# Half of the contraction of x @ w_ffn_in as 2x2 Strassen products in a float32 transformer trunk

## The chip, the cores and the metric

The kernel runs on one core of one Trainium2 chip. The metric is the device time of one execution in microseconds (us); lower is better. Engines: PE is TensorE's matmul stream, PEld its weight loads, DVE is VectorE, ACT is ScalarE, POOL is GpSimd, SP is SyncE, which here only issues transfers.

## The reference

Two layers of a streaming-encoder trunk on 256 tokens of width 2048, in float32. Each layer mixes tokens by three attention branches, merges them by gates, projects, normalizes, and then runs the feed-forward part:

```python
f_gate, f_up = jnp.split(x @ w_ffn_in[l], 2, axis=-1)      # w_ffn_in[l]: 2048 x 11264
x = layer_norm(DEEPNORM_ALPHA * x + (jax.nn.silu(f_gate) * f_up) @ w_ffn_out[l], ln2_g[l], ln2_b[l])
```

The hidden width is 5632, so `f_gate` and `f_up` are 11 chunks of 512 columns each.

## The kernel before

Every float32 product is made of three passes in float32r, TensorE's reduced float32 format: an operand w is split into h (w rounded) and l (w - h, rounded), and xh*wh + xh*wl + xl*wh accumulate in PSUM. One matmul takes 128 rows of the contraction (a k-tile), 128 tokens as the stationary operand and 512 weight columns as the moving one. The 256 tokens are two token tiles.

`gemm` computes 512 output columns for both token tiles in two PSUM banks. It goes over the contraction in units of two k-tiles. For each unit `load_unit` issues one transfer of 512 KB from DRAM on SP's queue into a `raw` buffer (5 of them), ACT rounds it into `wh` (L64) and DVE subtracts to get `wl` (L65); 6 buffers each of `wh` and `wl`. Then TensorE runs 12 matmuls of the unit (2 k-tiles x 2 token tiles x 3 passes, L90 to L92). A `gemm` over all 2048 rows is 8 units and 96 matmuls.

The feed-forward part goes over the 11 hidden chunks f in groups of 4, 4 and 3. For each f there is one `gemm` for the gate columns (L510), then sigmoid on ACT (L514) and a product on DVE (L515); one `gemm` for the up columns (L517), a product on DVE (L520), and 4 + 4 transposes on TensorE (L124, `hidTp`), split again into `rh` and `rl` (L52, L53). After a group, four `gemm`s multiply the hidden chunks by w_ffn_out. The text calls the gate `gemm` and the up `gemm` of one f, with what follows them, a **pair**: 192 matmuls and 8 transposes. There are 11 pairs in a layer and 22 in the kernel.

Each engine runs its instructions in the order in which they are put down; a scheduler sets that order when the program is built, and waits are semaphores. So an instruction that waits holds up everything behind it on its engine.

Of the kernel before, what the change touches and what calls it, by code (L numbers as in the profile page):

```python
# [29 lines left out]
UK = 2  # L30
# [3 lines left out]
def trunk_kernel(ctx: ExitStack, tc: tile.TileContext, x, w_in, sinks, lq1, lk1, lq2, lk2, diff_g,  # L34
                 rel_bias, w_br_a, w_br_b, w_br_c, w_gate, b_gate, w_out, ln1_g, ln1_b,
                 w_ffn_in, w_ffn_out, ln2_g, ln2_b, cos_a, sin_a, cos_b, sin_b, out):
    """Float32 products run as three float32r passes: w = h + l exactly, with h and l the
    float32r roundings of w and of w - h; xh*wh + xh*wl + xl*wh accumulate in PSUM."""
# [20 lines left out]
    def load_unit(src, k0, c0):  # L59
# [7 lines left out]

    side = []

    def pump():  # L70
        """one more stage of the work that runs beside the products"""
# [47 lines left out]
    def transpose4(src, name):  # L119
        """[128 tok, 4*128] -> PSUM [128, 4, 128 tok]"""  # L120
# [6 lines left out]
    # ---------------------------------------------------------------- constants  # L127
# [22 lines left out]
    # additive masks, [128 q, (keys of query tile 0: 128 | keys of query tile 1: 256)]  # L150
# [12 lines left out]
    for layer in range(DEPTH):  # L163
        lam_init = 0.8 - 0.6 * math.exp(-0.3 * layer)

        # ------------------------------------------------------------ q / k / v
        def head_slots(reg, i0, n):
            """n slots of [128, 256], two in each of the tiles reg{i0}, reg{i0+1}, .."""
# [3 lines left out]
        def rope(src, cos, sin, nh, hd):  # L172
            """src PSUM [128 tok, nh*hd] -> SBUF, rotated"""
# [45 lines left out]
        # ------------------------------------------------------------ attention of a pair of maps  # L219
        def exps(qs, ks, scale, bias, sk=None):  # L220
            """qs, ks: two [d, 256] operands, bias: additive, [128, 384] each; sk: sink columns.
            Returns exp(s - max) [128 q, 2, (k0 of q0 | k0 k1 of q1)] and the reciprocal sums [128, t, m]."""
            e = scr.tile([P, 2, 3 * P], F32, tag="e", name="e", bufs=2)
# [24 lines left out]
            return seg, rs  # L248
# [5 lines left out]
        def transposed(seg, n):  # L254
            """probabilities of n maps, key-major: [128 keys, n, 3, 128]: (q0,k0), (q1,k0), (q1,k1)"""
            pT = scr.tile([P, 2, 3, P], F32, tag="pT", name="pT", bufs=2)
# [6 lines left out]
            return pT  # L263

        def pv_heads(seg, rs, vs, yh, yl, i0):
# [3 lines left out]
            pT = transposed(seg, 2)  # L269
# [11 lines left out]
        def attn_a(h0, aq, ak, av, yh, yl):  # L281
            kv = h0 // 4
            seg, rs = exps([aq[h0], aq[h0 + 1]], [ak[kv]] * 2, P ** -0.5, [mask_a] * 2, slice(h0, h0 + 2))
            yield from pv_heads(seg, rs, [av[kv]] * 2, yh, yl, h0 % 4)

        def attn_c(h0, cq, ck, cv, yh, yl):
            seg, rs = exps([cq[h0], cq[h0 + 1]], [ck[h0], ck[h0 + 1]], P ** -0.5,
                           [relb[:, h0 + i, :] for i in range(2)])
            yield from pv_heads(seg, rs, [cv[h0], cv[h0 + 1]], yh, yl, h0)

        def attn_b(h, bq, bk, bv, yh, yl):
            seg, rs = exps([bq[h][0:64], bq[h][64:128]], [bk[h][0:64], bk[h][64:128]], 64 ** -0.5, [mask_b] * 2)
# [6 lines left out]
            pT = transposed(seg, 1)  # L299
# [27 lines left out]
        # ------------------------------------------------------------ branch A  # L327
# [11 lines left out]
        # ------------------------------------------------------------ small per-layer values  # L339
# [22 lines left out]
        # relb[p, h, :]: rel_bias[h, 256 + t - u] with the chunk mask, laid out as the masks.  # L362
        # raw[p, c] = rel_bias[h, 129 + p + c], so raw[p, 255 - c] = rel_bias[h, 384 + p - c].
# [21 lines left out]
        # ------------------------------------------------------------ branch B  # L385
# [9 lines left out]
        # ------------------------------------------------------------ branch C  # L395
# [10 lines left out]
        # ------------------------------------------------------------ gates, branch projections, merge  # L406
# [33 lines left out]
        # ------------------------------------------------------------ layer norm  # L440
# [27 lines left out]
        # ------------------------------------------------------------ output projection, residual, norm  # L468
# [25 lines left out]
        # ------------------------------------------------------------ feed-forward  # L494
# [10 lines left out]
        groups = [range(0, 4), range(4, 8), range(8, NFC)]  # L505
        stats = new_stats()
# [76 lines left out]
```

## Time and profile before

| | |
|---|---|
| Time, median of 3 runs | 2859.63 us (2859.13 to 2859.66) |
| Profiled execution, first to last instruction | 2858.1 us |
| Busy: PE, PEld | 2828.1 us, 2332.2 us |
| Busy: DVE, ACT, POOL | 1624.8 us, 1243.3 us, 60.5 us |
| Moved by DMA | 549.17 MB |
| Granted TensorE clock, mean | 0.999 |

The span of the profiled execution is 1.5 us short of the median of the runs; what lies around the span is start and end. PE's busy time is not a measure of its peak, since matmuls are pipelined and their ends are modelled: one matmul of 512 columns is recorded as some 390 ns, and the next starts long before it ends. How many matmuls start in a stretch says more.

### The profile page before, as it was taken

To read this page: it belongs to the slowest core of one execution; us is meant where nothing else is said; L and a number is where in the kernel's file an instruction comes from. 1 tells how busy PE (TensorE), PEld (TensorE's weight loads), DVE (VectorE), ACT (ScalarE), POOL (GpSimd) and SP (SyncE) were. 2 spreads that over 40 slices of the span, in tenths; PEclk is the share of its full clock that TensorE was granted. 3 is DMA by queue.
4 is the path that set the end of the run, shared out by engine and by line. 5 is a ranking of instruction groups with operands and counts; after the bars stand their busy time and mean duration, and the time that the engine had idled before them with its cause. 6 is when DMAs were issued, how large, how long until landed. Compare 5 with 4: busy or idle time off the path is not lost. (4 is left out here: it accounts for less than half of the span.)

```text
span 2858.1 us, 33530 instructions
## 1 busy us (share of the span) xinstructions
PE 2828.1 (99%) x12840; PEld 2332.2 (82%) x12840; DVE 1624.8 (57%) x1816; ACT 1243.3 (44%) x1590; POOL 60.5 (2%) x110
## 2 busy tenths in 40 slices
PE   8999999999999999999999999999999999999998
PEld 6888888887888888888878888888878888888886
DVE  5656556566555455555576565556575555554555
ACT  4455444443444444344345454444444434443442
POOL 0000000000000000000000000000000000000000
PEclk9999999999999999999999999999999999999999
DMA  7555666665655555566564556666656556555653
GB/s 252 170 162 174 206 201 202 198 226 175 219 190 192 192 190 190 191 190 198 183 214 152 179 180 199 203 201 206 212 198 191 190 191 195 186 190 192 192 191 125
DMA packets 282656, 549.17 MB, mean 192 GB/s; under 512 B 19840, under 2 KB 21376, under 8 KB 282496
## 3 DMA queue, kind: packets, MB, share of 16 engines
q1 hardware_dynamic: 276096, 526.07, 56.7%
q0 software_dynamic: 6400, 20.98, 2.5%
q8 instruction: 100, 1.64, 0.2%
q14 instruction: 60, 0.49, 0.0%
HBM read 542.78 MB, written 4.19 MB: 191 GB/s over the span
## 5 line engine op out<-in xcount | busy, mean ns | idle before, releaser
L65 DVE TENSOR_TENSOR wl<-raw,wh 128x1024 fp32r<-128x1024 f32 x992 | 1212.1, 1224 | 1129.3 <-ACT wh L64 1128.7
L64 ACT CAST wh<-raw 128x1024 fp32r<-128x1024 f32 x992 | 1044.7, 1054 | 1478.7 <-PE acc L92 1369.0
L90 PE MATMUL acc<-wh,xh 128*128 128x512 f32 x2752 | 1082.2, 393 | 8.4 <-ACT xh L52 8.3
L92 PE MATMUL acc<-wh,xl 128*128 128x512 f32 x2752 | 1076.1, 391 | 0.2 <-DVE xl L53 0.2
L91 PE MATMUL acc<-wl,xh 128*128 128x512 f32 x2752 | 1073.9, 390 | 2.1 <-DVE wl L65 1.9
L90 PEld LDWEIGHTS acc<-wh,xh 128*128 128x128 f32 x2752 | 517.5, 188 | 117.3 <-ACT xh L52 10.6
L91 PEld LDWEIGHTS acc<-wl,xh 128*128 128x128 f32 x2752 | 517.8, 188 | 109.5 <-DVE wl L65 4.7
L92 PEld LDWEIGHTS acc<-wh,xl 128*128 128x128 f32 x2752 | 517.4, 188 | 109.1 <-DVE xl L53 2.2
L92 PE MATMUL acc<-wh,rl 128*128 128x512 f32 x1216 | 474.4, 390 | 0.0
L90 PE MATMUL acc<-wh,rh 128*128 128x512 f32 x1216 | 474.2, 390 | 0.0
L91 PE MATMUL acc<-wl,rh 128*128 128x512 f32 x1216 | 473.5, 389 | 0.0
L92 PEld LDWEIGHTS acc<-wh,rl 128*128 128x128 f32 x1216 | 228.3, 188 | 47.3
L91 PEld LDWEIGHTS acc<-wl,rh 128*128 128x128 f32 x1216 | 228.3, 188 | 46.9
L90 PEld LDWEIGHTS acc<-wh,rh 128*128 128x128 f32 x1216 | 228.3, 188 | 46.9
L239 ACT ACTIVATE e<-e,nm 128x128 f32<-128x128 f32 (+1 forms) x80 | 35.4, 444 | 23.9 <-DVE nm L233 23.9
L459 POOL TENSOR_TENSOR rstd<-rstd,mhalf 128x1 f32<-128x1 f32 x8 | 7.7, 966 | 1585.6 <-DVE rstd L458 1585.6
L514 ACT ACTIVATE sig<-acc 128x512 f32<-128x512 f32 x44 | 26.3, 598 | 23.4 <-PE acc L92 21.6
L515 DVE TENSOR_TENSOR sig<-sig,acc 128x512 f32<-128x512 f32 x44 | 30.1, 688 | 7.8 <-ACT sig L514 7.8
L420 DVE TENSOR_TENSOR gate<-acc,bg 128x512 f32<-128x512 f32 x48 | 31.0, 683 | 1.2 <-PE oT L319 1.1
L52 ACT CAST xh<-xTp 128x512 fp32r<-128x512 f32 x32 | 17.7, 588 | 31.4 <-PE xTp L124 31.0
L53 DVE TENSOR_TENSOR rl<-hidTp,rh 128x512 fp32r<-128x512 f32 x44 | 28.2, 682 | 0.0
L520 DVE TENSOR_TENSOR sig<-sig,acc 128x512 f32<-128x512 f32 x44 | 28.1, 680 | 0.0
(123 smaller groups left out, 822.9 us busy)
## 6 DMA issues: line engine op xcount, KB each, us to landing
raw<-in_w_ffn_in_dram SPq DMA_DIRECT2D x352, 512.0 KB, 3.4
raw<-in_w_gate_dram SPq DMA_DIRECT2D x192, 512.0 KB, 4.3
raw<-in_w_ffn_out_dram SPq DMA_DIRECT2D x176, 512.0 KB, 3.5
raw<-in_w_in_dram SPq DMA_DIRECT2D x144, 512.0 KB, 3.6
raw<-in_w_out_dram SPq DMA_DIRECT2D x64, 512.0 KB, 4.0
raw<-in_w_br_a_dram SPq DMA_DIRECT2D x32, 512.0 KB, 4.1
raw<-in_w_br_b_dram SPq DMA_DIRECT2D x16, 512.0 KB, 4.7
raw<-in_w_br_c_dram SPq DMA_DIRECT2D x16, 512.0 KB, 4.8
```

Source lines behind the costliest of these rows:

```text
L52: nc.scalar.copy(h, src)
L53: nc.vector.tensor_sub(l, src, h.bitcast(F32))
L64: nc.scalar.copy(h, raw)
L65: nc.vector.tensor_sub(l, raw, h.bitcast(F32))
L90: nc.tensor.matmul(acc[t], ah, wh[:, j, :], start=kt == 0, stop=False)
L91: nc.tensor.matmul(acc[t], ah, wl[:, j, :], start=False, stop=False)
L92: nc.tensor.matmul(acc[t], al, wh[:, j, :], start=False, stop=kt == nk - 1)
L239: nc.scalar.activation(seg[t][:, m, :], seg[t][:, m, :], AF.Exp, bias=nm[:, t, m:m + 1], accum_out=sm[:, t, m:m + 1])
L420: nc.vector.tensor_add(g, acc[t], bg)
L514: nc.scalar.activation(s, accg[t], AF.Sigmoid)
L515: nc.vector.tensor_mul(s, s, accg[t])
L520: nc.vector.tensor_mul(sg[t], sg[t], accu[t])
```

## The change

For the pairs f = 1 to 10 of each layer (20 in all; f = 0 stays as it was) the two `gemm`s become one `pair_gemm`. It takes the gate columns N1 and the up columns N2 of the weights together, as the two column blocks of a 2x2 block product; the two token tiles are the two row blocks.

The contraction's 16 k-tiles are four chunks of 4. Chunks 0 and 2 (`cs`) go by the Winograd form of Strassen's product: 7 block products of 128 tokens x 2 k-tiles x 512 columns in place of 8. Chunks 1 and 3 (`cp`) go plainly (`four`), into the same PSUM banks, and where a bank holds a combination they use the sum that it calls for (one difference of token tiles per chunk). One chunk of each kind makes a **block** of the text; a pair is two blocks. TensorE works through the units of a block in this order, each with 6 matmuls, those written with "plain" 12:

u (u0, product p7), f1 (plain), p1, H1 (hub, q5), f2 (plain), p3 (b22), H2 (hub, p6), f3 (plain), p2, f4 (plain), H3 (hub, q4).

That is 11 units and 90 matmuls. The weight sums: `T` ("hub") is loaded on SP's queue, DVE adds it to b22 (`u0`, L599), and then three DMAs on POOL's queue with an add (`grow`, L603, 512 KB each) turn it into the next sums in place. A `grow` waits until DVE has read T for the product before; the split of T for the next product waits until the `grow` has landed. Two T buffers alternate between blocks.

The sums of x are made once per layer (`x_sums`), beside the plain pair f = 0. At the end of a pair seven DVE additions and one ACT copy turn seven PSUM banks into the four results; all eight banks are in use (four tags `acc`, four `aux`). The groups of hidden chunks are 3, 3, 3 and 2, in place of 4, 4 and 3. To make room, the buffers of the attention probabilities share one tag (`att`), which `u0` uses too, and the last `gemm`'s `tail` is 8 in both layers.

```diff
+    def block(src, k0, c0):
+        return src[k0 * P:(k0 + UK) * P, c0:c0 + CW].rearrange("(k p) n -> p k n", p=P)
+    def load_raw(src, k0, c0):
         raw = wpool.tile([P, UK, CW], F32, tag="raw", name="raw", bufs=5)
+        nc.sync.dma_start(raw, block(src, k0, c0))
+        return raw
+    def split_unit(raw):
         h = wpool.tile([P, UK, CW], F32R, tag="wh", name="wh", bufs=6)
         l = wpool.tile([P, UK, CW], F32R, tag="wl", name="wl", bufs=6)
-        nc.sync.dma_start(raw, src[k0 * P:(k0 + UK) * P, c0:c0 + CW].rearrange("(k p) n -> p k n", p=P))
         nc.scalar.copy(h, raw)
         nc.vector.tensor_sub(l, raw, h.bitcast(F32))
         return h, l
...
+        def pair_gemm(src, n1, n2):
+            bank = {}
+            for k in ("p3", "p7", "q5", "q4"):
+                bank[k] = psA.tile([P, CW], F32, tag="acc", name=k)
+            for k in ("p1", "p6", "p2"):
+                bank[k] = psX.tile([P, CW], F32, tag="aux", name=k)
...
+            def prod(k, lhs, w):
+                for j in range(UK):
+                    (ah, al), (wh, wl) = lhs(j), w
+                    nc.tensor.matmul(bank[k], ah, wh[:, j, :], start=k not in begun, stop=False)
+                    begun.add(k)
+                    nc.tensor.matmul(bank[k], ah, wl[:, j, :], start=False, stop=False)
+                    todo[k] -= 1
+                    nc.tensor.matmul(bank[k], al, wh[:, j, :], start=False, stop=todo[k] == 0)
...
+            for i in range(2):
+                cs, cp = 2 * i, 2 * i + 1
+                k1, k2, kp = 4 * cs, 4 * cs + 2, 4 * cp
...
+                T = act.tile([P, UK, CW], F32, tag=("rh3", "rl3")[i], name="hub")
+                nc.sync.dma_start(T, block(src, k1, n2))
+                b22 = load_raw(src, k2, n2)
+                u0 = scr.tile([P, UK, CW], F32, tag="att", name="u0", bufs=2)
+                nc.vector.tensor_add(u0, T, b22)
+                prod("p7", s3, split_unit(u0))
+                def grow(kr, c0):
+                    nc.gpsimd.dma_start(T, block(src, kr, c0), accum_op=ALU.add)
+                def four(j0, c0, ks):
+                    w = load_unit(src, kp + j0, c0)
+                    for k, (h, l) in ks:
+                        prod(k, part(h, l, j0), w)
...
+                N2 = (("q5", X[1]), ("p3", sums[cp][0]))
+                N1 = (("p2", X[0]), ("q4", X[1]))
+                grow(k1, n1)
+                four(0, n2, N2)
+                prod("p1", A[0][0], load_unit(src, k1, n1))
+                prod("q5", s1, split_unit(T))
+                grow(k2, n2)
+                four(2, n2, N2)
+                prod("p3", s4, split_unit(b22))
+                prod("p6", s2, split_unit(T))
+                grow(k2, n1)
+                four(0, n1, N1)
+                prod("p2", A[0][1], load_unit(src, k2, n1))
+                four(2, n1, N1)
+                prod("q4", A[1][1], split_unit(T))
+            p1, v, y, c22 = tmp("p1"), tmp("v"), tmp("y"), tmp("c22")
+            nc.scalar.copy(p1, bank["p1"])
+            nc.vector.tensor_sub(v, bank["p6"], p1)
+            nc.vector.tensor_sub(y, bank["p7"], v)
+            nc.vector.tensor_add(v, bank["q5"], v)
+            nc.vector.tensor_sub(c22, v, bank["p7"])
+            nc.vector.tensor_add(v, bank["p3"], v)
+            nc.vector.tensor_add(p1, bank["p2"], p1)
+            nc.vector.tensor_add(y, bank["q4"], y)
+            return [p1, y], [v, c22]
...
-        groups = [range(0, 4), range(4, 8), range(8, NFC)]
+        groups = [range(0, 3), range(3, 6), range(6, 9), range(9, NFC)]
...
+        side.append(x_sums())
...
-                accg = gemm(w_ffn_in[layer], 0, 16, f * CW, x_lhs)
                 sg = []
+                if f == 0:
+                    accg = gemm(w_ffn_in[layer], 0, 16, f * CW, x_lhs)
+                else:
+                    drain()
+                    accg, accu = pair_gemm(w_ffn_in[layer], f * CW, FFN + f * CW)
```

The order on the engines, at three places. First DVE at the seam between the pairs f = 1 and f = 2 of layer 0. Before, the splits (L65) of two `gemm`s follow on one another, with the two products L520 and the splits `rl1` of the hidden chunk between them:

```order
L65 TENSOR_TENSOR wl_6219<-raw_6217,wh_6218 128x1024
L65 TENSOR_TENSOR wl_6237<-raw_6235,wh_6236 128x1024
L520 TENSOR_TENSOR sig_5991<-sig_5991,acc_5997 128x512
L520 TENSOR_TENSOR sig_5994<-sig_5994,acc_5998 128x512
L65 TENSOR_TENSOR wl_6255<-raw_6253,wh_6254 128x1024
L53 TENSOR_TENSOR rl1_6144<-hidTp_6146,rh1_6143 128x4x128
L53 TENSOR_TENSOR rl1_6144<-hidTp_6154,rh1_6143 128x4x128
L65 TENSOR_TENSOR wl_6273<-raw_6271,wh_6272 128x1024
```

Now, from the last split of the first pair (H3, on `hub_6050`) to the one that waits for its last matmul (L635, on bank q4), the seven additions stand between the splits of the next pair's units u, f1, p1 and H1 (on `u0_6252`, `raw_6265`, `raw_6283`, `hub_6248`):

```order
L73 TENSOR_TENSOR wl_6196<-hub_6050,wh_6195 128x1024
L73 TENSOR_TENSOR wl_6255<-u0_6252,wh_6254 128x1024
L629 TENSOR_TENSOR v_6206<-p6_5893,p1_6205 128x512
L73 TENSOR_TENSOR wl_6268<-raw_6265,wh_6267 128x1024
L630 TENSOR_TENSOR y_6207<-p7_5889,v_6206 128x512
L631 TENSOR_TENSOR v_6206<-q5_5890,v_6206 128x512
L73 TENSOR_TENSOR wl_6286<-raw_6283,wh_6285 128x1024
L632 TENSOR_TENSOR c22_6208<-v_6206,p7_5889 128x512
L634 TENSOR_TENSOR p1_6205<-p2_5894,p1_6205 128x512
L633 TENSOR_TENSOR v_6206<-p3_5888,v_6206 128x512
L73 TENSOR_TENSOR wl_6296<-hub_6248,wh_6295 128x1024
L635 TENSOR_TENSOR y_6207<-q4_5891,y_6207 128x512
```

What moved: six of the seven additions and four splits of the next pair now stand ahead of the first instruction that needs the end of this pair.

Second, DVE inside a pair, after the seam. Before, only splits of freshly loaded `raw` tiles:

```order
L65 TENSOR_TENSOR wl_6273<-raw_6271,wh_6272 128x1024
L65 TENSOR_TENSOR wl_6291<-raw_6289,wh_6290 128x1024
L65 TENSOR_TENSOR wl_6317<-raw_6315,wh_6316 128x1024
L65 TENSOR_TENSOR wl_6335<-raw_6333,wh_6334 128x1024
L65 TENSOR_TENSOR wl_6353<-raw_6351,wh_6352 128x1024
```

Now, from the pair's first block after H2 (units f3, p2, f4) through its second block's H2 (on `hub_6403` the second time); L599 is the next block's `u0`:

```order
L73 TENSOR_TENSOR wl_6348<-raw_6345,wh_6347 128x1024
L73 TENSOR_TENSOR wl_6366<-raw_6363,wh_6365 128x1024
L73 TENSOR_TENSOR wl_6378<-raw_6375,wh_6377 128x1024
L599 TENSOR_TENSOR u0_6407<-hub_6403,raw_6405 128x1024
L73 TENSOR_TENSOR wl_6394<-hub_6248,wh_6393 128x1024
L73 TENSOR_TENSOR wl_6410<-u0_6407,wh_6409 128x1024
L73 TENSOR_TENSOR wl_6423<-raw_6420,wh_6422 128x1024
L73 TENSOR_TENSOR wl_6441<-raw_6438,wh_6440 128x1024
L73 TENSOR_TENSOR wl_6451<-hub_6403,wh_6450 128x1024
L73 TENSOR_TENSOR wl_6464<-raw_6461,wh_6463 128x1024
L73 TENSOR_TENSOR wl_6480<-raw_6405,wh_6479 128x1024
L73 TENSOR_TENSOR wl_6490<-hub_6403,wh_6489 128x1024
```

What moved: between the splits on one hub (`hub_6403`, H1 and then H2) there are two splits on `raw` tiles, and L599 stands ahead of the H3 of the block before it.

Third, SP's queue at the same pair. Before, one load for each unit, in the units' order:

```order
L63 DMA raw_6125<-in_w_ffn_in_dram 128x2x512
L63 DMA raw_6163<-in_w_ffn_in_dram 128x2x512
L63 DMA raw_6181<-in_w_ffn_in_dram 128x2x512
L63 DMA raw_6199<-in_w_ffn_in_dram 128x2x512
L63 DMA raw_6217<-in_w_ffn_in_dram 128x2x512
```

Now, from the second block's b22 (`raw_6052`) to the next pair's b22 (`raw_6250`); `hub_6248` is the next pair's first T:

```order
L66 DMA raw_6052<-in_w_ffn_in_dram 128x2x512
L66 DMA raw_6067<-in_w_ffn_in_dram 128x2x512
L66 DMA raw_6085<-in_w_ffn_in_dram 128x2x512
L66 DMA raw_6108<-in_w_ffn_in_dram 128x2x512
L66 DMA raw_6147<-in_w_ffn_in_dram 128x2x512
L596 DMA hub_6248<-in_w_ffn_in_dram 128x2x512
L66 DMA raw_6165<-in_w_ffn_in_dram 128x2x512
L66 DMA raw_6177<-in_w_ffn_in_dram 128x2x512
L66 DMA raw_6250<-in_w_ffn_in_dram 128x2x512
```

What moved: b22's `raw` buffer is free only after unit p3, and the fifth `raw` load behind it (`raw_6165`, unit p2) takes the same buffer, so that the loads of p2, of f4 and of the next b22 stand behind that wait.

## Rows read from the trace of the kernel before

**Rows 1.** The page, part 1: busy us (share of the span) and instructions.

```profile
PE 2828.1 (99%) x12840; PEld 2332.2 (82%) x12840; DVE 1624.8 (57%) x1816; ACT 1243.3 (44%) x1590; POOL 60.5 (2%) x110
```

**Rows 2.** Waits, whole span: engine, line, releaser: us in total, times, longest.

```profile
ACT wh L64 <- PE acc L92: 1369.0, 837, 5.7
DVE wl L65 <- ACT wh L64: 1128.7, 855, 7.3
...
PEld hidTp L124 <- DVE sig L520: 5.5, 22, 0.3
```

**Rows 3.** Timeline of PE in a w_ffn_out product: start us, us, engine, line.

```profile
1219.26 0.39 PE L91 MATMUL acc<-wl,rh 128*128 128x512 f32 x1
...
1221.98 0.39 PE L91 MATMUL acc<-wl,rh 128*128 128x512 f32 x1
```

**Rows 4.** Timeline of ACT, 717 to 858 us: the sigmoids, first and last of four.

```profile
723.16 1.28 ACT L514 ACTIVATE sig<-acc 128x512 f32<-128x512 f32 x2 [0.94 <-PE acc L92]
...
856.65 1.28 ACT L514 ACTIVATE sig<-acc 128x512 f32<-128x512 f32 x2 [0.98 <-PE acc L92]
```

**Rows 5.** The page, part 5: the costs of one split on DVE and ACT.

```profile
L65 DVE TENSOR_TENSOR wl<-raw,wh 128x1024 fp32r<-128x1024 f32 x992 | 1212.1, 1224 | 1129.3 <-ACT wh L64 1128.7
L64 ACT CAST wh<-raw 128x1024 fp32r<-128x1024 f32 x992 | 1044.7, 1054 | 1478.7 <-PE acc L92 1369.0
```

**Rows 6.** Timeline of DVE and ACT: instructions that follow on one another without a gap.

```profile
1708.00 2.35 DVE L65 TENSOR_TENSOR wl<-raw,wh 128x1024 fp32r<-128x1024 f32 x2
...
1209.90 1.28 DVE L536 TENSOR_TENSOR r<-r,acc 128x512 f32<-128x512 f32 x2
...
746.56 1.24 ACT L52 CAST rh<-hidTp 128x512 fp32r<-128x512 f32 x2
```

**Rows 7.** DMA answers for four short windows (574, 580, 608, 630 us): xres, median us to landing.

```profile
xres<-in_x_dram POOLq DMA_DIRECT2D x2, 256.0 KB, 7.7
xres<-in_x_dram POOLq DMA_DIRECT2D x2, 256.0 KB, 7.3
xres<-in_x_dram POOLq DMA_DIRECT2D x2, 256.0 KB, 4.8
xres<-in_x_dram POOLq DMA_DIRECT2D x2, 256.0 KB, 3.8
```

**Rows 8.** The same windows: busy us by engine (PE, PEld, DVE, ACT, POOL), PEclk, DMA share, GB/s.

```profile
574.00:576.00 2.00, 2.00 (x11) 1.65 (x10) 1.39 (x2) 1.47 (x3) 1.54 (x3) 1.00 0.86 243
580.00:582.00 2.00, 2.00 (x14) 1.55 (x13) 2.00 (x4) 0.94 (x2) 1.09 (x2) 1.00 0.98 288
608.00:610.00 2.00, 2.00 (x14) 1.54 (x13) 2.00 (x3) 0.84 (x3) 1.09 (x2) 1.00 0.69 240
630.00:632.00 2.00, 2.00 (x11) 1.65 (x10) 2.00 (x5) 0.96 (x1) 1.09 (x2) 1.00 0.61 201
```

**Rows 9.** xres by its tile: DMA, min, median and max.

```profile
DMA to landing us min/median/max: 3.8/4.9/7.9
```

**Rows 10.** DMA answers for 732 to 735 us and for 717 to 720 us: loads of weights.

```profile
raw<-in_w_ffn_in_dram SPq DMA_DIRECT2D x1, 512.0 KB, 3.3
raw<-in_w_ffn_in_dram SPq DMA_DIRECT2D x3, 512.0 KB, 5.6
```

**Rows 11.** The page, part 3: queue, kind: packets, MB, share of 16 engines.

```profile
q1 hardware_dynamic: 276096, 526.07, 56.7%
q0 software_dynamic: 6400, 20.98, 2.5%
```

**Rows 12.** Windows over one plain pair, columns as in Rows 8.

```profile
804.00:848.00 44.00, 44.00 (x199) 36.43 (x198) 22.86 (x23) 19.02 (x20) 0.00 (x0) 1.00 0.59 187
```

More of the change, by code (lines that the diff above doesn't have):

```diff
@@ L66, in load_unit @@
         return h, l
+    def load_unit(src, k0, c0):
+        return split_unit(load_raw(src, k0, c0))
     side = []
@@ L247, in exps @@
             nc.vector.reciprocal(rs, sm)
-            return seg, rs
+            return seg, rs, pT
         def wait(n):
@@ L268, in pv_heads @@
             yield from wait(3)
-            pT = transposed(seg, 2)
+            transposed(seg, pT, 2)
             yield
@@ L298, in attn_b @@
             yield from wait(3)
-            pT = transposed(seg, 1)
+            transposed(seg, pT, 1)
             yield
@@ L503, in finish, with sum_tile @@
                 nc.sync.dma_start(out[0, t * P:(t + 1) * P, c * CW:(c + 1) * CW], r[c][t])
-        groups = [range(0, 4), range(4, 8), range(8, NFC)]
+        sums = {}
+        def sum_tile(i, name):
+            if i < 6:
+                return act.tile([P, 4, P], F32R, tag=f"fa{i}", name=name)
+            if i < 8:
+                i -= 6
+                if i == 0:
+                    sums["pair"] = const.tile([P, 2, 4, P], F32R, tag="relb", name=name)
+                return sums["pair"][:, i]
+            return scr.tile([P, 4, P], F32R, tag="bc", name=name, bufs=4)
@@ new lines, in x_sums @@
+        def x_sums():
+            for c in range(NCH):
+                z = []
+                for t in range(NT):
+                    v = tmp("z").rearrange("p (k q) -> p k q", k=4)
+                    nc.vector.tensor_add(v, xh[c][t].bitcast(F32), xl[c][t].bitcast(F32))
+                    z.append(v)
+                if c % 2:
+                    nc.vector.tensor_sub(z[0], z[0], z[1])
+                    parts = [z[0]]
+                    i = 8 + c - 1
+                else:
+                    a11, a12, a21, a22 = (v[:, j:j + 2, :] for v in z for j in (0, 2))
+                    p, q = (tmp("zs").rearrange("p (k q) -> p k q", k=4) for _ in range(2))
+                    s1, s2, s3, s4 = p[:, 0:2], p[:, 2:4], q[:, 0:2], q[:, 2:4]
+                    nc.vector.tensor_sub(s1, a21, a22)
+                    nc.vector.tensor_sub(s3, a11, a21)
+                    nc.vector.tensor_sub(s2, a11, s1)
+                    nc.vector.tensor_sub(s4, a12, s2)
+                    parts = [p, q]
+                    i = 2 * c
+                yield
+                got = []
+                for v in parts:
+                    h, l = sum_tile(i, "sh"), sum_tile(i + 1, "sl")
+                    i += 2
+                    split(h, l, v)
+                    got.append((h, l))
+                sums[c] = got
+                yield
@@ L509, in trunk_kernel @@
             for f in grp:
-                accg = gemm(w_ffn_in[layer], 0, 16, f * CW, x_lhs)
                 sg = []
+                if f == 0:
+                    accg = gemm(w_ffn_in[layer], 0, 16, f * CW, x_lhs)
+                else:
+                    drain()
+                    accg, accu = pair_gemm(w_ffn_in[layer], f * CW, FFN + f * CW)
                 for t in range(NT):
@@ L516, in trunk_kernel @@
                     sg.append(s)
-                accu = gemm(w_ffn_in[layer], 0, 16, FFN + f * CW, x_lhs)
+                if f == 0:
+                    accu = gemm(w_ffn_in[layer], 0, 16, FFN + f * CW, x_lhs)
                 hc = ychunk(len(hid))
@@ L529, in trunk_kernel @@
                 acc = gemm(w_ffn_out[layer], 4 * grp[0], 4 * len(grp), c * CW, r_lhs(hid),
-                           tail=(8 if layer < DEPTH - 1 else 12) if last and c == NCH - 1 else 0)
+                           tail=8 if last and c == NCH - 1 else 0)
                 for t in range(NT):
```

28 lines of the change are left out of this document (17 added, 11 removed).

## The prediction

> **What bounds the kernel now.** I read the page's busy times first. PE is at 99% of the span, DVE at 57%, ACT at 44% [rows 1]. Since a busy PE is not PE at its peak, the waits come next. ACT waits for PE (its `wh` buffers come free) 1369.0 us, DVE waits for ACT 1128.7 us, and TensorE, at the end of all 22 pairs together, waits 5.5 us [rows 2]. So the feeders wait for TensorE and TensorE for nobody. In the timeline 12 matmuls start in 1221.98 - 1219.26 = 2.72 us, 0.2267 us each [rows 3], at a granted clock of 1.00 [rows 12]. Three pairs take 856.65 - 723.16 us, 44.5 each [rows 4]: 192 x 0.2267 = 43.5, and 1.0 for the 8 transposes. The time is the number of matmuls times their pitch, as long as DVE keeps ahead.
>
> **What is removed.** A pair has 180 matmuls in place of 192: 12 x 20 x 0.2267 = 54.4 us less. The kernel's own execution (span 2858.1 and 1.5 around it) is the median 2859.6, so with nothing else it would be 2805.2. A pair would last 41.8 us on PE with its transposes. The Strassen matmuls have the same shapes as the old ones, so I keep their pitch.
>
> **What is added on DVE and ACT.** One split is 1.22 us on DVE and 1.05 us on ACT when it stands alone [rows 5]; two in a row take 2.35, so I count 1.14 each; a 512-column operation 0.61 on DVE and 0.62 on ACT, from 1.28 and 1.24 for two [rows 6]. A pair now has 22 splits, 2 `u0` additions as large, and 13 small operations (7 additions, 4 products, 2 splits of the hidden chunk): 24 x 1.14 + 13 x 0.61 = 35.3 us on DVE, where it was busy 22.9 of 44 [rows 12]. ACT has 22 x 1.05 + 5 x 0.62 = 26.2 us. Both are below 41.8, so as sums of work they fit. DVE's slack is 6.5 us a pair.
>
> **What is added as waits: the grows.** No row shows an adding DMA. I call L the time from DVE's last read of T to the landing of the sum. Below: two plain 256 KB loads issued 0.55 us apart on POOL's queue landed in 3.8, so the 512 KB were there 4.4 after the first issue, at a DMA share of 0.61 [rows 7, 8]; a share of 0.69 gives 4.8 + 0.55 = 5.3. Above: the worst such load took 7.9 [rows 9]; the bursts at 0.86 and 0.98 gave 7.7 and 7.3 [rows 7, 8]. I take 5.3: the size is that of those two rows together, the queues here are between quiet and busy, and the fetching of what is added to, which has no row, keeps me off 4.4. The Trainium skill (page DMA: Bandwidth & Descriptors, section Anatomy of one DMA — SWDGE (gpsimd) path) puts a DMA from GpSimd at 2.0 us plus bytes over 436 GB/s, for 512 KB an estimate of 3.2; by that all grows are hidden and the time is 2805.2. The trace does not bear it out: half the size took at least 3.8 [rows 9].
>
> After landing comes ACT's cast, 1.05, so DVE goes on L + 1.1 = 6.4 us after its last read. Meanwhile only what stands in between in DVE's order is done. I count from the end of a split of H1.
>
> Second block of a pair: f2 and p3 end at 2.3, then DVE waits; H2 runs 6.4 to 7.5. `u0` needs the next b22, whose load is the third in the row that p3 releases on SP's queue: 3.3 for one load [rows 10] and 1.6 for each more (56.7% of 2858.1 us is 1620 us for 526.07 MB, so 1.62 per 512 KB [rows 11]) is 6.6; three loads at once had a median of 5.6 [rows 10]. So `u0` runs 8.9 to 10.0, f3, p2, f4 end at 13.4, H3 may start at 7.5 + 6.4 = 13.9 and ends at 15.1. Then the next pair's u, f1, p1 with six additions, 7.1: 22.2. H1 ends at 23.3.
>
> First block after a seam: the last addition, four products, f2 and p3 end at 5.3. ACT's order has H2's cast ahead of the hidden chunk's, so its splits run from 7.0 to 8.2 and H2 ends at 9.4; f3, p2, f4 12.8; `u0` 13.9; H3 at 9.4 + 6.4 = 15.8, done 16.9; u, f1, p1 20.4; H1 ends at 21.5.
>
> A pair on DVE is 21.5 + 23.3 = 44.8 us, of which 9.5 are waits, against 41.8 on PE: **3.0 us too many in a middle pair.** They become PE time only when DVE's lead is used up. With six `wh` buffers the cast of a group's first H1 starts when PE is done with the unit six before, two units (5.4 us) ahead of the group, and H1 ends 3.1 us ahead of it. The first block of a first pair has two additions of L536 in place of the seam's work: p3 ends at 3.5, `u0` at 3.5 + 6.6 + 1.1 = 11.2, f4 14.7, H3 15.8, p1 19.2, H1 20.4. So the second pair begins with H1 at -3.1 + 43.7 - 41.8 = -1.2, the third at -1.2 + 44.8 - 41.8 = 1.8. What PE meets first at a seam is a bank: p7's is free after c22, 20.9 into the second block; the `gemm` after a group needs p3's, free at 22.2. A last pair has it at 21.5 + 22.2 = 43.7 plus that start: 42.5 after two pairs (0.7 late), 45.5 after three (3.7 late). A middle pair has p7's at -1.2 + 42.4 = 41.2, in time. The changed pairs of a layer come in groups of 2, 3, 3 and 2: 2 x (2 x 3.7 + 2 x 0.7) = 17.6 us for both layers.
>
> Costed at nothing: the transposes (18 matmuls of the next pair, 4.1 us, stand ahead of them, and the first needs 3.6 us of DVE after the last matmul; without that cover some 3 us a pair); `x_sums` (13 us on DVE beside the plain pair f = 0, where DVE is free 21 of 44 us [rows 12]); one group more (8 additions, 5 us of DVE in a stage where it is half idle); T's own load (one block early on SP's queue).
>
> **Sum:** 2859.6 - 54.4 + 17.6 = **2823 us**. The same steps with other L: up to 4.4, 2805; 5.0, 2809 (a third pair is still 0.9 late, 3.6 in all); 6.0, 2873; 6.5, 2913; 7.9, 3025. So it turns at L = 5.8, and each 0.1 us beyond 5.2 costs some 7 us, since three of the six grows of a pair stand in DVE's line and there are 20 pairs.
>
> **Rivals.** *All hidden, 2805:* L below 5.0. For it: while the grow behind H1 is in flight, SP has little to issue, and the lightest window gave 4.4. Against it: that was a plain load, and it adds nothing.
>
> *The sums land late, slower, 2873 to 2925:* L of 6.0 to 6.6. VectorE's line becomes the bound: at 6.5 a middle pair is 49.6 us, longer than the 44.5 it replaces. For it: 7.3 to 7.7 for half the size beside bursts of loads [rows 7, 8], and p3's end releases such a burst (p2, f4, b22 and the next f1) just ahead of the grow behind H2. Against it: the four rows lie on both sides. It decides from 5.8.
>
> *The DMA engines fill up, slower, 2877 or more:* a pair moves 22 x 1.62 = 35.6 us of engine time in 41.8, a share of 0.85 where it was 0.58, near the windows' 0.86 that had the slow landings. If an added 512 KB occupies the engines twice, a pair needs 16 x 1.62 + 6 x 3.24 = 45.4 us, 0.9 more than 44.5, so 2859.6 + 18. By the Trainium skill (the same page, section Rules for kernel authors) an accumulating DMA reads its destination and writes it later; no run here shows what that costs.
>
> *Given back exactly:* L near 5.8 leaves the time where it was.
>
> **Chances.** The forecast (L 5.0 to 5.65, 2809 to 2850) 0.37; all hidden 0.19; landing late 0.28; engines full 0.09; given back 0.07. A change of 0.2% (5.7 us) is about what a measurement of this kernel can tell from none. Faster 0.37 + 0.19 = 0.56, same 0.07, slower 0.37. The range goes from 2803 to 2915: below it nothing is known, above it lie half of the late landings and half of the full engines, 0.18.
>
> **What would show it.** PE: 180 matmuls of 512 columns in a middle pair and a pitch of 0.2267 still; no long idle time inside a first pair of a group, some at the start of what follows a third (waiting for an addition on DVE, not for a split). DVE: busy 35 us a pair, its waits mostly ACT's cast of a hub, ACT's on a DMA from POOL's queue. DMA: hub from POOL some 5.2 us to landing, share 0.8 to 0.9 in a pair. I am wrong if the grows take over 5.8 us, if PE waits for `wl` inside a block, if DVE's operations lengthen beside POOL's descriptors, or if splits on `raw` tiles, and not on hubs, come late.

## The result, and the profile after

The changed kernel takes 3058.55 us (median of four runs, 3057.1 to 3061.3) against 2859.64 for the kernel before on the same chip: a ratio of 1.0696, 95% interval 1.0682 to 1.0711. It is 7% slower, where 2823 was forecast and the range ended at 2915. The profiled execution has a span of 3055.3 us and a mean granted clock of 0.978.

The page of the changed kernel, part 1, with the columns of [rows 1]:

```profile
span 3055.3 us, 34024 instructions
...
PE 2858.8 (94%) x12600; PEld 2316.0 (76%) x12600; DVE 1901.7 (62%) x2180; ACT 1354.1 (44%) x1742; POOL 206.3 (7%) x230
```

The 240 matmuls are gone (12840 before), and PE still has 196 us outside its busy time where it had 30. DVE is at 62% and ACT at 44%, so neither is the bound by its sum of work. The waits, with the columns of [rows 2], say who is late:

```profile
ACT wh L72 <- DMA hub<-in_w_ffn_in_dram: 501.6, 104, 9.9
...
PE hidTp L135 <- DVE sig L659: 42.6, 22, 3.3
PE p L580 <- ACT wh L72: 35.7, 14, 5.7
PE p L580 <- DVE v L631: 24.2, 12, 2.9
PE acc L101 <- DVE v L631: 22.5, 8, 2.9
```

ACT's cast of a hub, which the kernel before does not have, waits 104 times for a transfer, 4.8 us on average. TensorE, which waited for the feeders only 5.5 us at the ends of the pairs [rows 2], now waits for the products and additions of DVE and for hubs. The groups of instructions on hubs (busy, mean ns of one | idle time before them and what ended it):

```profile
L73 DVE TENSOR_TENSOR wl<-hub,wh 128x1024 fp32r<-128x1024 f32 x120 | 146.8, 1224 | 377.6 <-ACT wh L72 377.3
L72 ACT CAST wh<-hub 128x1024 fp32r<-128x1024 f32 x120 | 126.0, 1050 | 545.5 <-DMA hub<-in_w_ffn_in_dram 501.6
...
L603 POOL DMA_DIRECT2D hub<-in_w_ffn_in_dram x120 | 145.3, 1228 | 1374.2 <-DVE wl L73 865.4
```

The splits themselves cost what they did [rows 5]; DVE stands 377.6 us in front of 120 of them. DVE's timeline in one pair shows the line that the prediction reckoned with:

```profile
827.57 1.23 DVE L73 TENSOR_TENSOR wl<-hub,wh 128x1024 fp32r<-128x1024 f32 x1
828.72 2.35 DVE L73 TENSOR_TENSOR wl<-raw,wh 128x1024 fp32r<-128x1024 f32 x2
837.82 1.23 DVE L73 TENSOR_TENSOR wl<-hub,wh 128x1024 fp32r<-128x1024 f32 x1 [6.75 <-ACT wh L72]
838.96 3.49 DVE L73 TENSOR_TENSOR wl<-raw,wh 128x1024 fp32r<-128x1024 f32 x3
848.57 1.23 DVE L73 TENSOR_TENSOR wl<-hub,wh 128x1024 fp32r<-128x1024 f32 x1 [6.12 <-ACT wh L72]
```

These are H1, f2 and p3, H2, then f3, p2, f4, then H3. From H1's end (827.57 + 1.23 = 828.80) to H2's start it is 9.0 us; without the cast (1.1) that is **L = 7.9** for the grow behind H1. From H2's end (839.05) to H3 it is 9.5, so L = 8.4. ACT's cast of a hub waits for the transfer in both cases. The prediction had 5.3.

The sigmoids at the end of two pairs on ACT, as in [rows 4]:

```profile
968.84 0.64 ACT L652 ACTIVATE sig<-p 128x512 f32<-128x512 f32 x1 [1.77 <-DVE p L634]
...
1023.24 0.63 ACT L652 ACTIVATE sig<-p 128x512 f32<-128x512 f32 x1 [2.01 <-DVE p L634]
```

This pair lasts 54.4 us where a pair lasted 44.5; the twelve such distances inside groups go from 52.8 to 61.2, with a mean of 56.5. Transfers (part 3 as in [rows 11], and the issues: KB each, median us to landing):

```profile
q1 hardware_dynamic: 276096, 526.07, 53.8%
q0 software_dynamic: 39040, 83.90, 14.8%
...
raw<-in_w_ffn_in_dram SPq DMA_DIRECT2D x312, 512.0 KB, 5.5
...
hub<-in_w_ffn_in_dram POOLq DMA_DIRECT2D x120, 512.0 KB, 7.9
```

The adding transfers took (14.8% of 3055.3) - (2.5% of 2858.1 [rows 11]) = 381 us of the engines for 120 x 512 KB: 3.17 us each, where a plain 512 KB on SP's queue costs 1.62.

### The profile page after: what moved, and what is told of

It reads as the page before. It is cut to its first block, busy times and chain, and to the rows that moved or that the text cites. A ratio compares the mean times of both kernels' runs of the same rounds, so it can differ in the third digit from the quotient of the medians.

```text
span 3055.3 us, 34024 instructions
## 1 busy us (share of the span) xinstructions
PE 2858.8 (94%) x12600; PEld 2316.0 (76%) x12600; DVE 1901.7 (62%) x2180; ACT 1354.1 (44%) x1742; POOL 206.3 (7%) x230
## 3 DMA queue, kind: packets, MB, share of 16 engines
q0 software_dynamic: 39040, 83.90, 14.8%
q8 instruction: 99, 1.62, 0.2%
## 5 line engine op out<-in xcount | busy, mean ns | idle before, releaser
L101 PE MATMUL acc<-wh,xh 128*128 128x512 f32 x1472 | 583.1, 397 | 7.9 <-ACT xh L54 7.9
L102 PE MATMUL acc<-wl,xh 128*128 128x512 f32 x1472 | 576.8, 392 | 11.4 <-DVE wl L73 11.3
L103 PE MATMUL acc<-wh,xl 128*128 128x512 f32 x1472 | 576.8, 392 | 0.2 <-DVE xl L55 0.2
L73 DVE TENSOR_TENSOR wl<-hub,wh 128x1024 fp32r<-128x1024 f32 x120 | 146.8, 1224 | 377.6 <-ACT wh L72 377.3
L102 PEld LDWEIGHTS acc<-wl,xh 128*128 128x128 f32 x1472 | 277.6, 189 | 70.3 <-DVE wl L73 15.0
L101 PEld LDWEIGHTS acc<-wh,xh 128*128 128x128 f32 x1472 | 277.7, 189 | 67.7 <-ACT xh L54 10.2
L103 PEld LDWEIGHTS acc<-wh,xl 128*128 128x128 f32 x1472 | 277.5, 188 | 59.5 <-DVE xl L55 2.2
L603 POOL DMA_DIRECT2D hub<-in_w_ffn_in_dram x120 | 145.3, 1228 | 1374.2 <-DVE wl L73 865.4
L580 PE MATMUL p<-wh,sh 128*128 128x512 f32 x400 | 162.9, 407 | 59.9 <-ACT wh L72 35.7
L582 PE MATMUL p<-wl,sh 128*128 128x512 f32 x400 | 163.0, 407 | 10.2 <-DVE wl L73 10.2
L582 PE MATMUL q<-wl,xh 128*128 128x512 f32 x400 | 159.6, 399 | 9.0 <-DVE wl L73 9.0
L580 PE MATMUL q<-wh,xh 128*128 128x512 f32 x400 | 160.3, 401 | 4.8 <-ACT wh L72 3.8
```

What stands on the lines that cost most here:

```text
L73: nc.vector.tensor_sub(l, raw, h.bitcast(F32))
L101: nc.tensor.matmul(acc[t], ah, wh[:, j, :], start=kt == 0, stop=False)
L102: nc.tensor.matmul(acc[t], ah, wl[:, j, :], start=False, stop=False)
L103: nc.tensor.matmul(acc[t], al, wh[:, j, :], start=False, stop=kt == nk - 1)
L580: nc.tensor.matmul(bank[k], ah, wh[:, j, :], start=k not in begun, stop=False)
L582: nc.tensor.matmul(bank[k], ah, wl[:, j, :], start=False, stop=False)
```

## The experiments

Three theories stood for the lost 236 us (3058.6 against 2822.6, the time of the best of the first kernels below with the same matmuls and sums). **A:** the sum lands some 8 us after the last read of T, and three of the six grows of a pair stand in DVE's line, which becomes the bound. **B:** the added work itself (24 large operations and the seams, a lower clock) costs the time, whenever the sums land. **C:** the DMA engines are full, because an adding transfer occupies them twice. Single times are of one run beside one run of the kernel before; those with an interval were timed in rounds.

**No grows, fresh loads.** All matmuls, splits and seams stay; each hub split takes a block of its own through the weight loader, so the hubs hold single weight blocks and not sums.

```diff
-                grow(k1, n1)
-                prod("q5", s1, split_unit(T))
-                grow(k2, n2)
+                prod("q5", s1, load_unit(src, k1, n1))
...
-                prod("p6", s2, split_unit(T))
-                grow(k2, n1)
+                prod("p6", s2, load_unit(src, k2, n2))
...
-                prod("q4", A[1][1], split_unit(T))
+                prod("q4", A[1][1], load_unit(src, k2, n1))
```

> The three adding DMAs of a block are left out, and each hub split reads a freshly loaded block of weights in its place (three plain loads more on SP's queue; the sums of weights are left out). Theory A (the adding DMAs land some 7.9 us after the last read, and that wait stands in VectorE's line): no such wait is left, a pair has 35 us of VectorE work against 41.8 us of TensorE, so 2805 to 2825 us. Theory B (the added work, the banks handed over at the seams and the clock cost the time, whatever the landing): 2900 us or more. Theory C (the DMA engines are full): 22 loads a pair are 35.6 us of engine time in 41.8, so loads come late still and it stays above 2840 us.

Measured 2827.47 us (before: 2858.77). The three sigmoids that end pairs of the second group stand at 939.42, 981.80 and 1023.34: 42.4 and 41.5 us a pair. So the added splits, additions and seams fit beside 180 matmuls as forecast (41.8), and B falls as the main cause; nor do 22 plain loads a pair fill the DMA engines.

**Plain copies in place of the adds.** The same 120 transfers on GpSimd's queue into the same T with the same waits, but they copy; the hubs are single weight blocks.

```diff
-                    nc.gpsimd.dma_start(T, block(src, kr, c0), accum_op=ALU.add)
+                    nc.gpsimd.dma_start(T, block(src, kr, c0))
```

> The three DMAs of a block on POOL's queue stay, with all their waits, but copy in place of adding (the sums of weights are left out). If the add makes the landing long: 5.3 to 6.0 us to landing and 2823 to 2873 us, by the line of VectorE worked out before. If POOL's queue path itself is that slow for 512 KB: 7.5 us or more to landing and 3040 to 3060 us.

Measured 2872.72 us, 186 less than with the add. Its queue on the page, part 3:

```profile
q0 software_dynamic: 23680, 83.90, 10.0%
```

The wait of the casts of hubs:

```profile
ACT wh L72 <- DMA hub<-in_w_ffn_in_dram: 219.1, 74, 7.3
```

The issues:

```profile
hub<-in_w_ffn_in_dram POOLq DMA_DIRECT2D x120, 512.0 KB, 4.4
```

The split of H1 on DVE and the cast of H2 on ACT in one pair:

```profile
813.33 1.23 DVE L73 TENSOR_TENSOR wl<-hub,wh 128x1024 fp32r<-128x1024 f32 x1 [1.59 <-ACT wh L72]
819.66 1.05 ACT L72 CAST wh<-hub 128x1024 fp32r<-128x1024 f32 x1 [4.46 <-DMA hub<-in_w_ffn_in_dram]
```

The landing is 4.4 us, which is the quiet end of my bounds [rows 7], though the DMA share in these pairs is 0.77 to 0.81. In one pair (795 to 840 us) L, from a split's end to the next hub's cast, is 5.1 for the grow behind H1 (814.56 to 819.66) and 4.7 behind H2, but 6.5 behind `u0`. A plain copy took (10.0% of 2870.9) - (2.5% of 2858.1) over 120, or 1.80 us, of the engines. The adding itself, then, is most of the loss: 186 of 236 us. But 2873 is also some 60 us more than the table of the prediction gives for L = 5.1 (about 2814): the table was too kind to seams and to the grow behind `u0`.

**One grow left out.** First the second grow (behind H1), then the first (behind `u0`) alone; the hubs after it then hold other sums.

```diff
                 prod("q5", s1, split_unit(T))
-                grow(k2, n2)
```

```diff
                 prod("p7", s3, split_unit(u0))
...
-                grow(k1, n1)
                 four(0, n2, N2)
```

> The adding DMA ahead of H2 (the second of three in a block) is left out, so H2 splits the hub as H1 left it (one addend is missing from the sums). Theory A: VectorE has only two splits between H1 and H2, so this is the grow that costs most; with L = 7.9 us a middle pair goes from 55.2 to 46.0 us and the time to about 2840 us. Theory C (engine time of the adding DMAs): one third of the adding DMAs is gone, so about one third of the loss, 2985 to 3000 us.

> The adding DMA ahead of H1 (the first of three in a block) is left out in place of the second (one addend is missing from the sums). Theory A: between u0 and H1 VectorE has 16 us of other work and waits already, so H1 never waits for this grow: about 3045 to 3060 us, as with it. Theory C: one third of the adding DMAs is gone, 2985 to 3000 us, the same as without the second.

Measured 2890.11 without the second and 3016.08 without the first: 168 us and 42 us less than 3058. The two remove the same bytes and the same engine time, so a cost by bytes alone (C) would have made them equal; it is the place in DVE's line that counts. Neither number was A's, though (2840; 3045 to 3060): the first grow is not free, and with two grows in a block part of the loss remains. Medians of the landing, place by place, are 10.5, 7.1 and 7.8 us for the three grows of a block in the changed kernel, 8.4 and 6.3 for the first and third without the second, and 6.1 and 6.9 for the second and third without the first. Where the row of grows is thinned out, the rest land sooner, so contention is in L too.

**The price of an add by itself.** The kernel before, with 44 more 512 KB transfers on GpSimd's queue into a tile that nobody reads, by turns adding (L516) and plain (L518), each behind the last. One buffer of `wl` (5 in place of 6) makes room for the tile.

```diff
+                nc.gpsimd.dma_start(spare, block(w_ffn_in[layer], 0, f * CW), accum_op=ALU.add)
                 accg = gemm(w_ffn_in[layer], 0, 16, f * CW, x_lhs)
+                nc.gpsimd.dma_start(spare, block(w_out[layer], 0, f % NCH * CW))
```

> The kernel before, with 44 DMAs of 512 KB more on POOL's queue into one spare tile that nothing reads, in turn an adding one (from w_ffn_in) and a plain one (from w_out), each issued when the last has landed, beside the first part of layer 0. It measures the landing by itself, at a DMA share of about 0.6 from the loads. If the add is what takes long: adding 6.5 to 8 us, plain 4.5 to 5.5. If waiting behind other loads in the pairs made them long: adding below 6 us here. Time 2860 to 2875 us, since nothing waits for them but a few gate biases.

The groups of the two kinds (busy, mean ns of one | idle before them):

```profile
L516 POOL DMA_DIRECT2D spare<-in_w_ffn_in_dram x22 | 26.3, 1193 | 99.2 <-DMA spare<-in_w_out_dram 99.2
L518 POOL DMA_DIRECT2D spare<-in_w_out_dram x22 | 16.1, 734 | 138.1 <-DMA spare<-in_w_ffn_in_dram 138.1
```

Their issues, with the median us to landing:

```profile
spare<-in_w_ffn_in_dram POOLq DMA_DIRECT2D x22, 512.0 KB, 6.7
spare<-in_w_out_dram POOLq DMA_DIRECT2D x22, 512.0 KB, 5.1
```

With one of them at a time in flight the adding one lands in 6.7 us and the plain one in 5.1, and its issue holds GpSimd 1.19 us, not 0.73. All 44 ran in the first 290 us of the kernel, at DMA shares from 0.92 (20 to 100 us) down to 0.47 (222 to 284 us). In that last window no other data moved:

```profile
spare<-in_w_out_dram POOLq DMA_DIRECT2D x6, 512.0 KB, 3.9
spare<-in_w_ffn_in_dram POOLq DMA_DIRECT2D x6, 512.0 KB, 5.8
```

So by itself the add puts 1.9 us on the landing (0.5 of them at the issue), and in the pairs, against the plain copies in its place, 3.5 (7.9 and 4.4). The other 1.6 come where adding transfers and loads meet; no run shows which of them delays which. The time, 2951.6, missed the forecast: the chain of extra transfers stood in GpSimd's order ahead of a small power (`ors`) in the first layer's attention, for which DVE waited 86.5 us at once. It is no price of the adding.

**The sums on VectorE.** All results are computed. The raw blocks that p1, p3 and p2 load anyway are added into T by DVE, with no adding transfer:

```diff
-                def grow(kr, c0):
-                    nc.gpsimd.dma_start(T, block(src, kr, c0), accum_op=ALU.add)
+                def grow(raw):
+                    nc.vector.tensor_add(T, T, raw)
...
-                grow(k1, n1)
+                r11 = load_raw(src, k1, n1)
+                grow(r11)
...
-                prod("p1", A[0][0], load_unit(src, k1, n1))
+                prod("p1", A[0][0], split_unit(r11))
...
-                grow(k2, n2)
+                grow(b22)
```

and `r21` for p2 in the same way.

> All of the kernel's results are computed. The three sums of a block are made by VectorE additions into the hub, from the raw blocks that p1, p3 and p2 load anyway, so there is no adding DMA and six loads a pair fewer. Theory A: VectorE has 30 large operations and 13 small ones a pair, 30 x 1.14 + 13 x 0.61 = 42.1 us against 41.8 on TensorE, and few waits: 2815 to 2860 us. Theory B (work and seams cost the time): VectorE has more work than with adding DMAs, so above 3000 us.

Measured 2822.61 us (2821.0 to 2827.64), ratio 0.9872 (0.9858 to 0.9887): faster than both kernels. Its groups on hubs:

```profile
L73 DVE TENSOR_TENSOR wl<-hub,wh 128x1024 fp32r<-128x1024 f32 x120 | 146.8, 1224 | 19.9 <-ACT wh L72 18.0
L603 DVE TENSOR_TENSOR hub<-hub,raw 128x1024 f32<-128x1024 f32 x120 | 146.7, 1223 | 3.5 <-DMA raw<-in_w_ffn_in_dram 2.1
```

DVE does 147 us more work and waits 358 us less in front of hubs. The sigmoids of the first two changed pairs stand at 790.33 and 832.07, 41.74 us apart, and the next three at 939.10, 982.53 and 1023.35, on average 42.1 apart, where 41.8 was forecast for a pair that PE bounds.

**The same sums on GpSimd.** As above, with `nc.gpsimd.tensor_add`.

> All of the kernel's results are computed. The same, with the three additions on GpSimd in place of VectorE. No run shows what such an addition takes on GpSimd; it has time for 6 in 41.8 us up to 7 us each. Theory A: if one lands within 4 us of VectorE's last read, all of it is hidden, 2805 to 2815 us; at 6 us about 2870 us; VectorE's splits longer than 1.14 us in a row would show that the two engines disturb each other.

Measured 2892.44 us, ratio 1.0111 (1.0095 to 1.0128). One addition takes GpSimd 2.6 us on average. Two rows of DVE's timeline and one of GpSimd's:

```profile
811.86 1.21 DVE L73 TENSOR_TENSOR wl<-hub,wh 128x1024 fp32r<-128x1024 f32 x1
813.14 3.28 DVE L73 TENSOR_TENSOR wl<-u,wh 128x1024 fp32r<-128x1024 f32 x1
812.02 3.31 POOL L603 TENSOR_TENSOR hub<-hub,raw 128x1024 f32<-128x1024 f32 x1 [4.57 <-DVE u L599]
```

The second has the form and size of the first and takes 3.28 us in place of 1.21, beside GpSimd's addition. Over the run this form on `u0` has a mean of 1694 ns, against 1224 for splits of hubs in the kernel with VectorE's adds, and the first two distances of sigmoids inside groups are 45.0 and 47.5 us. VectorE is busy 2086.6 us here and 2044.0 with its own adds, although 147 us of additions have left it. Moving the adds to an idle engine lengthened the work of the busy one.

**The sums of x later.** The kernel with VectorE's adds reaches 2822.6, not 2805. Its sigmoid of the plain pair f = 0 stands at 728.99, where that of before stands at 723.16 [rows 4], so the first loss comes ahead of all changed pairs. Here `x_sums` lets six units of f = 0 pass first:

```diff
         def x_sums():
+            for _ in range(6):
+                yield
             for c in range(NCH):
```

> The kernel with VectorE's adds in place of the adding transfers (2822.6 us), but the sums of x begin six units later in the pair f = 0. If the sums of x cost about 6 us in each of the two layers because they delay the first weight splits after the layer norm, as the later sigmoid of f = 0 says: 2810 us, between 2807 and 2814, and that sigmoid comes about 6 us earlier than at 729. If what is missing from 2805 lies in the pairs and their seams instead: 2820 to 2824, no change.

Measured 2808.01 us (2807.7 to 2811.92), ratio 0.9823 (0.9809 to 0.9838), the best of all. The first sigmoid of f = 0 in ACT's timeline:

```profile
721.60 1.28 ACT L656 ACTIVATE sig<-acc 128x512 f32<-128x512 f32 x2 [0.94 <-PE acc L103]
```

TensorE's wait for `wl` of plain products:

```profile
PE acc L102 <- DVE wl L73: 1.9, 3, 0.7
```

In the changed kernel the sigmoid and the wait are these:

```profile
729.25 1.08 ACT L652 ACTIVATE sig<-acc 128x512 f32<-128x512 f32 x2
```

```profile
PE acc L102 <- DVE wl L73: 11.3, 6, 2.7
```

So `x_sums` stood among the first weight splits after the layer norm, and this cost some 14 us in the two layers (14.6 between the two medians, 14.0 by the two ratios).

**Two blocks interleaved, same adding transfers.** What would the grows cost with cover enough? The units of a pair's two blocks alternate, so that some 11 us of other matmuls stand between a grow and its split (7 to 8 for the grow behind u; T's plain load moves to GpSimd's queue, and p3 follows u):

```diff
+            both = steps(0), steps(1)
+            for step in ("0u 0p3 0f1 0p1 1u 1p3 0H1 1f1 1p1 1H1 0f2 1f2 0H2 0f3 0p2 1H2 0f4 1f3 "
+                         "0H3 1p2 1f4 1H3").split():
+                both[int(step[0])][step[1:]]()
```

> The same adding transfers and the same matmuls as the changed kernel, but the units of a pair's two blocks are interleaved, so that a hub's sum has about 11 us of other matmuls ahead of its split instead of 4 (and the two plain loads of a hub go out on GpSimd's queue, so that they hold up no weight load). If only the landing counts (theory A): pairs of 41.7 to 42.5 us and 2820 to 2840 us. If the DMA engines are full (theory C): 16 loads at 1.62 us and 6 adding ones at 3.17 us are 44.9 us of every pair, so pairs of 45 us or more and 2885 us or more. If the added work itself costs the time (theory B): above 2990 us.

Measured 2852.97 us, ratio 0.998 (0.9971 to 0.999): 206 of the 236 us come back with every adding transfer in place. That is A, but 2820 to 2840 is not reached. The sigmoids that end two pairs:

```profile
942.38 0.63 ACT L662 ACTIVATE sig<-p 128x512 f32<-128x512 f32 x1 [1.12 <-DVE p L644]
...
987.78 0.63 ACT L662 ACTIVATE sig<-p 128x512 f32<-128x512 f32 x1 [1.95 <-DVE p L644]
```

A window inside a group, with the columns of [rows 8], and behind it the issues of hubs (the 40 plain loads of T among them):

```profile
810.00:830.00 20.00, 20.00 (x90) 16.55 (x89) 13.22 (x13) 12.34 (x14) 3.78 (x4) 1.00 1.07 311
```

```profile
hub<-in_w_ffn_in_dram POOLq DMA_DIRECT2D x160, 512.0 KB, 7.1
```

From the one sigmoid to the other it is 45.4 us (45.2 and 44.7 in this layer's other pairs up to f = 5), and C's sum was 16 x 1.62 + 6 x 3.17 = 44.9. In the window of 20 us the share is 1.07 (packet times can overlap). But over a whole pair it is less:

```profile
942.00:987.00 45.00, 45.00 (x204) 37.12 (x202) 35.28 (x37) 24.33 (x27) 8.77 (x8) 1.00 0.95 256
987.00:1032.00 45.00, 41.79 (x182) 34.14 (x181) 36.02 (x39) 25.63 (x28) 7.49 (x7) 0.96 0.92 262
```

And of the loads it is only the grows that a cast waits for there (the waits from 942 to 988 us have no `raw`):

```profile
ACT wh L72 <- DMA hub<-in_w_ffn_in_dram: 9.4, 3, 5.6
```

So C's number fits, but it is not shown that full engines set the 45 us: the landing, 5.6 to 10.1 us for the adding transfers here, still stands in DVE's line in places (A). TensorE starts 204 matmuls in the first window and 182 in the second, so what is late reaches it only at the end of a group, and the price is 30 us and not C's 62.

**The same with plain copies.** To tell C from a price of the interleaved order, the adds are left out of it, as in the second experiment (the hubs hold single blocks).

```diff
-                    nc.gpsimd.dma_start(o["T"], block(src, kr, c0), accum_op=ALU.add)
+                    nc.gpsimd.dma_start(o["T"], block(src, kr, c0))
```

> The kernel with interleaved blocks, where each of the 120 adding transfers becomes a plain copy into the same place, with the same waits (the hubs then hold single weight blocks, not sums). It tells where the 30 us come from that the interleaved kernel (2853) takes more than the one with VectorE's adds (2822.6). If they are the engine time of the adding (6 x 3.17 + 16 x 1.62 = 44.9 us per pair, as its pairs of 45 us suggest), a plain copy needs 22 x 1.62 = 35.6 us per pair and the time goes to 2818 to 2828, pairs of 41.5 to 42.5 us. If they are the price of the interleaved order, its loads on GpSimd's queue or its seams: 2845 to 2853.

Measured 2820.38 us, ratio 0.9867 (0.985 to 0.9883). The same window:

```profile
810.00:830.00 20.00, 20.00 (x90) 16.57 (x89) 15.25 (x15) 11.35 (x11) 2.17 (x3) 1.00 0.89 299
```

Two sigmoids:

```profile
938.41 0.63 ACT L662 ACTIVATE sig<-p 128x512 f32<-128x512 f32 x1 [1.12 <-DVE p L644]
980.21 0.63 ACT L662 ACTIVATE sig<-p 128x512 f32<-128x512 f32 x1 [1.12 <-DVE p L644]
```

The share is 0.89 in this window, and 0.82 from 942 to 987 us. From the one sigmoid to the other it is 41.8 us (43.3 in this layer's other pairs up to f = 5). So the 33 us between the two kernels are the adding's: its longer use of the engines or its longer landing (the hubs' median is 5.0 us here and 7.1 with the adds), which this pair of runs does not separate. The interleaved order itself shows no cost.

**Interleaved, with the sums of x later.** The delay of the best kernel in the interleaved one with adding transfers.

> The interleaved blocks with the adding transfers, and the sums of x six units later. 10 to 12 us below the interleaved kernel by the theory that the sums of x delay the first splits of a layer, in the same place by the other.

Measured 2848.61 us, ratio 0.9961 (0.9947 to 0.9975): 4.4 less, not 10 to 12. In the first layer the sigmoid of f = 0 comes 6.6 us sooner than in the interleaved kernel (723.99 and 730.60), and the one that ends the first changed pair only 3.3 (788.40 and 791.70): a gain ahead of pairs that wait for transfers is partly lost in them again.

## Why the prediction was wrong

**What held.** The removed work: with the waits gone a pair lasts about 42 us (in the kernel with VectorE's adds the twelve distances of sigmoids inside groups go from 40.8 to 44.9 with a mean of 42.2; 41.8 was forecast), and the best kernel is at 2808 where "all hidden" was 2805. DVE's sum: the pair of 54.4 us shown above has 35.6 us of DVE (35.3). The mechanism: the wait is ACT's cast of a hub on a DMA from GpSimd's queue, DVE stands behind it, and TensorE first waits at the seams for additions. The line with L = 7.9 gave 3025; the grows at 7.9 to 8.4 gave 3058. That the two are so near is in part luck, since the same line was some 60 us too low at L = 5.1 and 50 too low without the second grow.

**The step that failed is the size of L.** I took 5.3, from two plain 256 KB loads, and kept "off 4.4" by 0.9 for the whole act of adding. Measured: a plain 512 KB in place lands in 4.4 us and makes L about 5; the adding one lands in 7.9 and makes L 7.9 to 8.4. Of these 3.5 us the add by itself is 1.9, of which 0.5 is a longer issue; the rest comes with the crowd in the pairs. The rows of before that I set aside as the upper bound, 7.3 to 7.7 at shares of 0.86 to 0.98 [rows 7, 8], have nearly the right number, but for another reason: those were plain loads in a burst, and plain copies in the pairs landed in 4.4 at shares near 0.8. What was missing was a row of an adding transfer. At some 7 us for each 0.1 of L, a value near a lower bound that came from rows without an add was the wrong choice. "Landing late" deserved the larger chance, and its own bounds went up to 7.9 and so to 3025: the range was cut at 2915 by halving that case.

**The rule cited.** The Trainium skill (page DMA: Bandwidth & Descriptors, section Anatomy of one DMA — SWDGE (gpsimd) path) gave 3.2 us for 512 KB. No kernel here has it: 3.9 for a plain copy with no other data moving, 4.4 into T, 5.0 to 5.1 in two others, 7.9 for the adding one. The Trainium skill's rule (the same page, section Rules for kernel authors), that an accumulating DMA reads its destination and writes it later, agrees with the longer engine time, 3.17 against 1.80 us for the plain copy in its place.

**The rival "engines full"** is not what bounds the changed kernel: its pairs, 52.8 us and more, are longer than the 45.4 forecast for it, and leaving out different grows with the same bytes gave different times. In the interleaved kernel pairs of 44.7 to 45.4 agree with it, but at a share of 0.92 to 0.95 and with hubs still landing late; whether it or the landing costs those 30 us is open.

**Costed at nothing, and wrong:** `x_sums`, some 14 us. DVE is free for half of the pair f = 0, as I said, but not at its start, where the splits are late after the layer norm. **Too kind:** the table between 5 and 6. The plain copies with L about 5.1 took 2873, not 2814: the grow behind `u0` (L 6.5), the transposes (TensorE waits 24.1 us for the `sig` that they read) and `x_sums` count too. Nor do only three of the six grows of a pair count: without the first ones of the blocks the changed kernel is 42 us faster. How the 60 us divide between these was not tried.

**The clock** is a term that I had not in the sum. After such a wait TensorE runs slower for a while; PE's timeline in the changed kernel:

```profile
854.14 0.47 PE L101 MATMUL acc<-wh,rh 128*128 128x512 f32 x1 [2.86 <-DVE v L631]
...
856.79 0.63 PE L103 MATMUL acc<-wh,rl 128*128 128x512 f32 x1
857.22 0.63 PE L101 MATMUL acc<-wh,rh 128*128 128x512 f32 x1
857.65 0.63 PE L102 MATMUL acc<-wl,rh 128*128 128x512 f32 x1
```

The starts are 0.43 us apart, twice the 0.2267 of [rows 3], so this is the lower level (1.2 GHz); it came after a wait of 2.86 and another of 0.71, and the granted clock of 850 to 860 us is 0.83. The mean went from 0.999 to 0.978, and it is 0.996 in the kernel with VectorE's adds. As an estimate from these means, 0.022 x 3055 = 67 us of full-speed time are missing in the one and 0.004 x 2826 = 11 in the other, so at most some 56 of the 236 us, if all of it lay on the path. In these rows the lower level follows the waits; how much it adds to them no run parts.

## What to carry to other kernels

An accumulating DMA is cheap for the engine that no longer adds and dear in other ways: it holds the DMA engines longer (3.17 us against 1.62 to 1.80) and lands later (7.9 against 4.4), so a chain that reads its result wants, as an estimate from L, 8 to 9 us or more of other work per 512 KB in between. Even with 7 to 11 us of it, in the interleaved kernel, the casts of hubs still waited 133 us in all for their transfers, where they had waited 502. If an operand of the sum is loaded anyway, an add on a VectorE with slack (1.22 us for 128 x 1024) beats it (2822.6 us against 3058.6, and 2853.0 interleaved), and a bound from loads that do not add is not a bound for one that does. Look for slack where the work is put, not on the average of the stage: 13 us of VectorE work a layer in a half-idle stage cost some 7 us a layer until it began six units later.

## What the runs showed of the hardware

- An adding 512 KB transfer took 3.17 us of engine time where a plain copy in its place took 1.80 (1.62 on SP's queue), and landed in 7.9 us (median) where that landed in 4.4. One at a time, with no other data moving, it was 5.8 against 3.9. It held GpSimd 1.19 us at its issue against 0.73.
- A GpSimd addition of 128 x 1024 took 2.6 us (mean), and VectorE operations of that size, 1.21 us elsewhere, took up to 3.39 us in that kernel.
- A chain of transfers on GpSimd's queue whose data nobody reads delayed a small GpSimd operation that stood behind it in the order, and with it VectorE by 86.5 us at once.
